# A decoder layer whose steps of attention and output projection are recorded in one block of manual order instead of two

## The chip, the core and the metric

The kernel runs on one core of a Trainium2 chip. A core has five engines with a queue of instructions each: PE (TensorE, matrix products; its weight loads are shown as PEld), DVE (VectorE), ACT (ScalarE), POOL (GpSimd) and SP (SyncE, which here only issues DMAs). An engine works its queue strictly in order and stands while the front instruction waits for a semaphore of another engine or of a DMA. The metric is the device time of one execution in microseconds (us).

## What is computed

One decoder layer in float32, 512 tokens of width 1024: a normalised input projection, two kinds of attention side by side, one output projection over both, a residual, and a SwiGLU feed-forward with its residual. Cut to its frame:

```python
for l in range(DEPTH):                                  # DEPTH = 1
    h = rms_norm(x, attn_pre_norm[l])
    mix = hybrid_mixer(h, ...)
    x = x + rms_norm(mix, attn_post_norm[l])
    h = rms_norm(x, ffn_pre_norm[l])
    f = (jax.nn.silu(h @ w_gate[l]) * (h @ w_up[l])) @ w_down[l]
    x = x + rms_norm(f, ffn_post_norm[l])

def hybrid_mixer(h, ...):
    dq, dk, dv, nq, kc, vc, ks, vs, kw, vw, gt = jnp.split(h @ w_in, ...)
    o_diff = ...        # 4 heads: difference of two causal softmaxes, then rms_norm
    o_nsa = nsa_attention(...)   # 8 heads: compressed, selected and window branch, mixed by gates
    return jnp.concatenate([o_diff, o_nsa], axis=-1) @ w_out
```

With 512 tokens the selected and the window branch of the second kind cover all causal keys.

## The kernel before

Every product is made to float32 accuracy from halves: a value is split into a high part (`h`, `hi`: ACT or POOL rounds it) and a low part (`l`, `lo`: DVE or POOL subtracts the high part from the value), and PE sums high x high, low x high and high x low. Tokens are worked in four blocks of 128.

The work is cut into small steps with names, and two tables of these names set the order in which the steps are recorded. `PLAN` holds the input projection and both attentions, head by head. Of a head of the second kind (`nsa_head`, names from `N0` to `N7`) the last steps are: `T` transposes the probabilities on PE (tile `tr`), `H` and `L` split them (`pth` on ACT, `ptl` on DVE), and `V1u` multiplies them with the values (`avs`, L1044, tile `avn`; `u` is 0, 1, 2, and unit 0 is the first key block, unit 1 the second, unit 2 the third and fourth). When the last matmul of `avn` is through, `O1` copies half of it (`avt`, ACT L1052), `O2` adds the two halves into `opair` (DVE L1058), `OH` makes the high part `oh` (ACT L1064) and `OL` the low part `ol` (POOL L1067). `D3OH` and `D3OL` do the same for head 3 of the first kind (ACT L958, POOL L974). `PLAN` ends with these steps of head 7.

`PLAN_NORM` holds what follows: the output projection in pieces (`mx20` is token block 2, row block 0 of the weight `w_out`: six matmuls `mix`, L1125, three for each half of the width), then for each token block its sum (`mixt`, DVE L1231), the norms and the residual `x` (ACT L1239, DVE L1254 to L1267), the scaled input of the feed-forward (`pre`, DVE L1271), its transposes on PE (`trh`, L1301) and the split of these (`x11h`, `x11l`, `x12h`, `x12l`). After it come the products of the feed-forward (`yz` and `x`, L1378), seven for eight by a scheme that multiplies sums of blocks, which is why DVE makes sums of weights first: `U1` (`e`, L1335), `U3` (`wraw`, L1342), `U2` (`e`, L1337), `U4` (`d`, L1340), then the low parts `wbl` and `wel` (L1363). Weights come by `load_w` (L267) into three buffers `wraw`; a load is issued by SP when the buffer's last reader is done.

`PLAN_NORM` begins with the loads of two weights and the pieces `mx20` and `mx30`, which need only attention heads that ended long before.

Each table is recorded inside a `manual_schedule()` of its own. Within such a block each engine gets its instructions in the order of the table. Where one block ends and the next begins, the two are not kept apart by anything but the data: the scheduler of the language puts the end of one and the start of the next into PE's queue as it sees fit. Between the two blocks the memory of the attention (`tctx`) is given back and the pools of the feed-forward are opened.

Of the kernel before, what the change touches and what calls it, by code (L numbers as in the profile page):

```python
# [245 lines left out]
def hybrid_block_kernel(  # L246
# [99 lines left out]
    ops = {}  # L346
# [813 lines left out]
        op(f"G{m}", mix_keep, m)  # L1160
    plan = PLAN.split()
    assert sorted(plan) == sorted(ops), set(plan) ^ set(ops)
    with tc.manual_schedule():
        for tok in plan:
            ops[tok]()
    tctx.close()
    A = ctx.enter_context(tc.tile_pool(name="a", bufs=1, side="right", reuse_waits="tile"))
    B = ctx.enter_context(tc.tile_pool(name="b", bufs=1, side="right", reuse_waits="tile"))
# [632 lines left out]
    plan, end = PLAN_NORM.split(), PLAN_END.split()  # L1801
    plan += [tok for _, tok in sorted(todo, key=lambda x: x[0]) if tok not in set(plan + end)] + end
    assert sorted(plan) == sorted(ops), set(plan) ^ set(ops)
    with tc.manual_schedule():
        for tok in plan:
            ops[tok]()


# [89 lines left out]
```

## Time and profile before

| what | value |
|---|---|
| three runs | 654.22, 1542.87 and 651.18 us; median 654.22 |
| profiled execution | 649.97 us, of which the span of instructions is 648.0 |
| granted clock of PE over the span | 0.995 |
| instructions | 11131, of which PE 4162 matmuls, DVE 955, ACT 780, POOL 151 |
| DMA | 98.42 MB, mean 152 GB/s |
| attention's last `opair` | 269.87 us from the span's start |
| feed-forward products on PE | 304 to 640 us |

The page shows one execution. Starts are counted from the span's start. "Idle before" is time in which an engine stood with its next instruction not yet released; the releaser named is the event that came last.

### The profile page before, as it was taken

How to read it: one execution, taken by the hardware profiler on the slowest of the kernel's cores; microseconds unless marked ns; L12 is line 12 of the kernel's file. 1: busy time of each engine (PE TensorE's matmuls, PEld its weight loads, DVE VectorE, ACT ScalarE, POOL GpSimd, SP SyncE). 2: the span in 40 equal slices, each digit the busy share in tenths (PEclk: the TensorE clock that was granted, in tenths of full speed). 3: DMA queues.
4: the chain of work that ended last, by engine and by line, in shares of the span. 5: the costliest groups of instructions: out<-in, count | busy, mean ns of one | idle time of the engine just before them, and what ended most of it. 6: DMA issues, size and time to landing. Idle time of an engine off the chain costs nothing.

```text
span 648.0 us, 11131 instructions
## 1 busy us (share of the span) xinstructions
PE 630.6 (97%) x4162; PEld 570.6 (88%) x4162; DVE 551.0 (85%) x955; ACT 374.3 (58%) x780; POOL 98.4 (15%) x151
## 2 busy tenths in 40 slices
PE   9999999999999999989999999999999999999995
PEld 6988787889998989868999999999999997778883
DVE  5799787688789776698999999988989999889886
ACT  7346545457787867557665735455554654657532
POOL 0200000006676787600000000000000000000000
PEclk9999999999999999989999999999999999999998
DMA  8467795257330321544235343334443365445722
GB/s 291 155 221 257 252 324 188 93 182 257 102 113 23 127 66 34 195 160 165 97 100 163 102 127 125 120 115 121 145 129 128 107 202 157 170 149 185 254 78 98
DMA packets 33045, 98.42 MB, mean 152 GB/s; under 512 B 4192, under 2 KB 5344, under 8 KB 32096
## 3 DMA queue, kind: packets, MB, share of 16 engines
q1 hardware_dynamic: 32992, 97.72, 45.1%
q8 instruction: 33, 0.54, 0.3%
q14 instruction: 20, 0.16, 0.1%
HBM read 82.10 MB, written 15.60 MB: 151 GB/s over the span
## 4 chain that ended last, share of the span: by engine, by line
PE 45%; DVE 8%; DMA 3%; ACT 1%; issue 1%; DVEq 0%; SPq 0%
PE yz L1378 27%; PE acc L1452 8%; PE x L1378 4%; PE acc L1600 3%; DMA wraw<-in_wd 2%; PE mix L1125 2%; DVE tl L1495 1%; DVE wraw L1469 1%; DVE wlo L1507 1%; DVE sl L1486 1%; DVE wraw L1471 1%; PE trh L1301 1%; DMA wraw<-in_wg 1%; ACT pre L1239 1%; DVE t L1475 1%
## 5 line engine op out<-in xcount | busy, mean ns | idle before, releaser
L848 ACT ACTIVATE p<-sc,nm 128x256 f32<-128x256 f32 (+3 forms) x96 | 50.1, 528 | 19.5 <-DVE nm L844 17.8
L844 DVE TENSOR_REDUCE nm<-sc 128x1 f32<-128x128 f32 (+3 forms) x96 | 43.3, 482 | 10.2 <-PE sc L840 6.9
L1378 PE MATMUL yz<-rope,wbh 128*128 128x256 f32 x352 | 49.1, 282 | 0.0
L1013 POOL TENSOR_TENSOR p<-p,l 128x256 f32<-128x256 f32 (+3 forms) x64 | 45.1, 729 | 0.9
L1378 PEld LDWEIGHTS yz<-rope,wbh 128*128 128x128 f32 x352 | 44.8, 188 | 0.3
L878 DVE TENSOR_TENSOR ptl<-tr,pth 128x384 fp32r<-128x384 f32 (+1 forms) x60 | 34.5, 594 | 8.7 <-ACT pth L875 8.1
L834 PE MATMUL sc<-kst,qst 128*128 128x384 f32 (+3 forms) x96 | 32.6, 357 | 2.9 <-DMA kst<-qk 2.1
L1355 ACT ACTIVATE weh<-e 128x1024 fp32r<-128x1024 f32 x22 | 23.3, 1057 | 19.7 <-DVE e L1337 17.0
L875 ACT ACTIVATE pth<-tr 128x384 fp32r<-128x384 f32 (+1 forms) x60 | 30.4, 526 | 6.6 <-PE tr L865 5.7
L835 PE MATMUL sc<-kst,qst 128*128 128x384 f32 (+3 forms) x96 | 30.9, 322 | 0.0
L1501 ACT ACTIVATE whi<-wraw 128x1024 fp32r<-128x1024 f32 x20 | 21.0, 1055 | 16.5 <-PE acc L1452 10.6
L1355 ACT ACTIVATE wbh<-wraw 128x1024 fp32r<-128x1024 f32 x22 | 23.1, 1056 | 11.5 <-DVE wraw L1342 11.4
L865 PE MATMUL tr<-ident,p 128*128 128x128 f32 x200 | 28.3, 274 | 0.0
L1363 DVE TENSOR_TENSOR wel<-e,weh 128x1024 fp32r<-128x1024 f32 x22 | 26.9, 1223 | 1.6 <-ACT weh L1355 1.6
L1363 DVE TENSOR_TENSOR wbl<-wraw,wbh 128x1024 fp32r<-128x1024 f32 x22 | 26.8, 1222 | 1.6 <-ACT wbh L1355 1.6
L1378 PE MATMUL yz<-rope,wbl 128*128 128x256 f32 x176 | 28.1, 282 | 0.0
L521 PE MATMUL fm<-xh,whi 128*128 128x512 f32 x112 | 28.0, 391 | 0.0
L1507 DVE TENSOR_TENSOR wlo<-wraw,whi 128x1024 fp32r<-128x1024 f32 x20 | 24.3, 1220 | 4.3 <-ACT whi L1501 4.3
L521 PE MATMUL fm<-xh,wlo 128*128 128x512 f32 x112 | 27.7, 390 | 0.0
L521 PE MATMUL fm<-xl,whi 128*128 128x512 f32 x112 | 27.7, 390 | 0.0
L1363 DVE TENSOR_TENSOR wlo<-wraw,whi 128x1024 fp32r<-128x1024 f32 x22 | 26.7, 1218 | 0.1
L1355 ACT ACTIVATE whi<-wraw 128x1024 fp32r<-128x1024 f32 x22 | 23.2, 1056 | 5.2 <-DMA wraw<-in_wg 4.7
(377 smaller groups left out, 1985.1 us busy)
## 6 DMA issues: line engine op xcount, KB each, us to landing
wraw<-in_wg SPq DMA_DIRECT2D x24, 512.0 KB, 3.6
wraw<-in_wu SPq DMA_DIRECT2D x22, 512.0 KB, 3.5
wraw<-in_wd SPq DMA_DIRECT2D x22, 512.0 KB, 4.0
wraw<-in_wf SPq DMA_DIRECT2D x14, 512.0 KB, 5.1
qk<-rope SPq DMA_DIRECT2D x7, 1024.0 KB, 4.9
kst<-qk SPq DMA_DIRECT2D x24, 256.0 KB, 3.8
wraw<-in_wo SPq DMA_DIRECT2D x8, 512.0 KB, 4.3
qst<-qk SPq DMA_DIRECT2D x16, 256.0 KB, 3.0
```

Of the source, the lines that this page charges most:

```text
L521: pe.matmul(st["fm", m], fms[m][w][:, k * P:(k + 1) * P], xx[k], start=(c == 0 and k == 0), stop=(c == 2 and k == NK - 1))
L834: pe.matmul(sv[i], lhs, kk[:, 0, :w], start=(n == 0), stop=False, skip_group_check=True)
L835: pe.matmul(sv[i], lhs, kk[:, 1, :w], start=False, stop=False, skip_group_check=True)
L844: dve.tensor_reduce(nm[i], sv[i], AX.X, OP.max, negate=True)
L848: act.activation(pp[i], sv[i], AF.Exp, bias=nm[i], accum_out=hs["l"][:, row, i:i + 1])
L878: dve.tensor_tensor(part(u, 1), tv[u], f32(part(u, 0)), OP.subtract)
L1013: pool.tensor_tensor(p, p, hs["l"][:, 1 + br, i:i + 1].to_broadcast(list(p.shape)), OP.mult)
L1355: act.activation(t[0], w[src], AF.Copy)
L1363: dve.tensor_tensor(t[1], W[f][PARTS[n][0]], f32(t[0]), OP.subtract)
L1378: pe.matmul(o, W[f][w][wi][:, k * P:(k + 1) * P], hop[h][hi][:, k * HS:(k + 1) * HS], start=(n < 3 and m == 0), stop=(m == 11), skip_group ...
L1452: pe.matmul(acc[t], a[x][:, t * P:(t + 1) * P], b[y], start=(first and n == 0), stop=(last and n == 2))
L1507: dve.tensor_tensor(lo, o["raw"], f32(o["w"][0]), OP.subtract)
```

## The change

The first `with tc.manual_schedule()` becomes a context of the whole function, so that it stays open to the kernel's end, and the second one is dropped. The tables, the steps and their code are the same.

```diff
     plan = PLAN.split()
     assert sorted(plan) == sorted(ops), set(plan) ^ set(ops)
-    with tc.manual_schedule():
-        for tok in plan:
-            ops[tok]()
+    ctx.enter_context(tc.manual_schedule())
+    for tok in plan:
+        ops[tok]()
     tctx.close()
...
     assert sorted(plan) == sorted(ops), set(plan) ^ set(ops)
-    with tc.manual_schedule():
-        for tok in plan:
-            ops[tok]()
+    for tok in plan:
+        ops[tok]()
```

What it does to the queues is seen only on PE, at the one place where the two tables meet. `avn` is the product of head 7 with the values (`vn_1541`, `vn_1573` and `vn_1551` are the values of the second, third and fourth key block), `mix` the output projection. PE's queue there before:

```order
L1125 MATMUL mix<-wl_432,oh_1985 128x512
L1044 MATMUL avn<-pth,vn_1541 128x384
L1125 MATMUL mix<-wh_428,oh_1985 128x512
L1125 MATMUL mix<-wh_428,ol_1986 128x512
L1125 MATMUL mix<-wl_469,oh_1985 128x512
L1044 MATMUL avn<-ptl,vn_1541 128x384
L1044 MATMUL avn<-pth,vn_1573 128x256
```

Ahead of these rows stand five more rows of `mix`, and behind them six, and then the last three of `avn`:

```order
L1044 MATMUL avn<-ptl,vn_1573 128x256
L1044 MATMUL avn<-pth,vn_1551 128x128
L1044 MATMUL avn<-ptl,vn_1551 128x128
L1125 MATMUL mix<-wh_3136,oh_3286 128x512
L1125 MATMUL mix<-wh_3136,ol_3287 128x512
```

PE's queue there now, from the spreading of head 3's norm (`rsb`) on:

```order
L953 MATMUL rsb<-ident,dr 128x128 x4
L1044 MATMUL avn<-pth,vn_1541 128x384
L1044 MATMUL avn<-ptl,vn_1541 128x384
L1044 MATMUL avn<-pth,vn_1573 128x256
L1044 MATMUL avn<-ptl,vn_1573 128x256
L1044 MATMUL avn<-pth,vn_1551 128x128
L1044 MATMUL avn<-ptl,vn_1551 128x128
L1125 MATMUL mix<-wh_428,oh_1985 128x512
L1125 MATMUL mix<-wh_428,ol_1986 128x512
```

The six `avn` now follow each other. The fifteen `mix` matmuls that stood ahead of and among them (six, three and six) come behind them, in the order they had. Everything behind is the same. The queues of DVE, ACT, POOL and SP hold the same instructions in the same order; here is DVE's, which reads what PE makes there:

```order
L972 TENSOR_TENSOR sq<-o_3499,rsb 128x512
L1058 TENSOR_TENSOR opair<-avn,avt 64x512
L1335 TENSOR_TENSOR e<-wraw 128x512
L1342 TENSOR_TENSOR wraw<-wraw 128x512
L1337 TENSOR_TENSOR e<-wraw,e 128x512
```

Nothing moved in DVE's rows. A few tiles take another buffer of the same size than before, and with it four waits name another instruction: `ol` of head 3 on POOL waits for the second `avn` of the six instead of the eighth `mix` matmul; `d` (L1340) waits also for a `mix` matmul of the piece `mx30`; and two loads deep in the feed-forward's second half exchange a wait for POOL.

## Prediction

> **What bounds the kernel now.** I read the page's table of engines first, then PE's own list of waits, then the chain of waits, and last the timelines of the engines around 260 to 310 us, where the change lies. Columns of a timeline row: start and duration in us, engine, line, operation, output<-input, shape, count, and in brackets the idle time ahead of it with its releaser.
>
> ```profile
> PE 630.6 (97%) x4162; PEld 570.6 (88%) x4162; DVE 551.0 (85%) x955; ACT 374.3 (58%) x780; POOL 98.4 (15%) x151
> ...
> PE trh L1301 <- ACT cols L1244: 2.4, 1, 2.4
> ...
> 286.03 1.82 PE L1301 MATMUL trh<-ident,pre 128*128 128x128 f32 x8 [2.44 <-ACT cols L1244]
> ```
>
> PE is busy 97% of the span, so a gain must come out of the little time in which PE stands, or in which it runs slowly. The longest single stand is the second row: 2.44 us ahead of the transposes `trh` of the first token block, ending at 286.03. This is 20 us behind the place that the change touches. The stand ends when DVE delivers `pre`; the operands come from DVE's queue, which is in one line from the end of attention to there:
>
> ```profile
> 263.75 1.00 DVE L878 TENSOR_TENSOR ptl<-tr,pth 128x384 fp32r<-128x384 f32 x2
> ...
> 269.87 0.68 DVE L1058 TENSOR_TENSOR opair<-avn,avt 64x512 f32<-64x512 f32 x1 [4.16 <-ACT avt L1052]
> 270.59 0.69 DVE L1335 TENSOR_TENSOR e<-wraw 128x512 f32<-128x512 f32 x1
> 271.37 1.77 DVE L1342 TENSOR_TENSOR wraw<-wraw 128x512 f32<-128x512 f32 x1
> ...
> 276.66 1.28 DVE L1231 TENSOR_TENSOR mixt<-mix,rope 128x512 f32<-128x512 f32 x2
> ...
> 279.36 0.69 DVE L1335 TENSOR_TENSOR e<-wraw 128x512 f32<-128x512 f32 x1 [0.16 <-DMA wraw<-in_wg]
> ...
> 285.13 0.75 DVE L1271 SCALAR_TENSOR_TENSOR pre<-x,cols,gain 128x512 f32<-128x512 f32 x1
> ...
> 285.86 0.74 DVE L1271 SCALAR_TENSOR_TENSOR pre<-x,cols,gain 128x512 f32<-128x512 f32 x1
> ```
>
> DVE stands 4.16 us ahead of `opair` (269.87) and then has work with hardly a break until `pre` (the two halves end at 285.88 and 286.60). So DVE's start at 269.87 decides when PE may go on at 286.03. What it stands for is ACT's `avt`, and that waits for the last `avn` matmul on PE:
>
> ```profile
> 265.75 0.63 ACT L958 ACTIVATE oh<-sq 128x512 fp32r<-128x512 f32 x1 [1.31 <-DVE sq L972]
> 269.24 0.60 ACT L1052 ACTIVATE avt<-avn 64x512 f32<-64x512 f32 x1 [2.86 <-PE avn L1044]
> ...
> 264.68 0.47 PE L1125 MATMUL mix<-wh,oh 128*128 128x512 f32 x1
> ...
> 266.15 0.34 PE L1044 MATMUL avn<-pth,vn 128*128 128x384 f32 x1
> 266.32 0.39 PE L1125 MATMUL mix<-wh,oh 128*128 128x512 f32 x1
> ...
> 268.70 0.28 PE L1044 MATMUL avn<-ptl,vn 128*128 128x256 f32 x1
> ...
> 268.98 0.45 PE L1125 MATMUL mix<-wh,oh 128*128 128x512 f32 x1
> ...
> 272.68 0.47 PE L1125 MATMUL mix<-wh,ol 128*128 128x512 f32 x1
> ```
>
> PE itself never stands here: between the six remaining `avn` matmuls it does 15 `mix` matmuls of the output projection.
>
> **The change, step by step.** No instruction is added or removed. On PE the six `avn` matmuls of head 7 move ahead of the 15 `mix` matmuls that stood among them; the order on DVE, ACT, POOL and in SP's queue stays row for row, so no DMA is moved.
>
> *PE's order itself: 0.* The first of the six holds PE 0.17 us (266.15 to 266.32), the last three 0.28 (268.70 to 268.98); with the two between, of the same shapes (0.17 and 0.12), about 0.74. They run 264.68 to 265.4, their last result is there at about 265.6, and the 15 `mix` matmuls go later by what the `avn` before them take, 0.74 at most. At 268.98 both orders have done the same work. The block needs the second `ptl` of DVE, done at 263.75 + 1.00 = 264.75; it is wanted at about 265.1, so PE does not stand. This cover is 0.4 us wide; before, the wanted time was 268.70.
>
> *`avt` and `opair`: 2.8 us earlier.* ACT has `oh` in front of `avt` (265.75 + 0.63 = 266.38), which is now what is late. `avt` goes at about 266.4 instead of 269.24, and `opair` at 267.0 to 267.7 instead of 269.87 to 270.55.
>
> *DVE against POOL: 2.6 to 4.0.* Two subtractions of weights follow `opair`, `e` and `wraw`, each with both inputs in SBUF.
>
> ```profile
> 265.45 1.30 POOL L1099 TENSOR_TENSOR wl<-wraw,wh 128x512 fp32r<-128x512 f32 x1
> 267.10 1.29 POOL L974 TENSOR_TENSOR ol<-sq,oh 128x512 fp32r<-128x512 f32 x1 [0.35 <-PE mix L1125]
> 271.30 1.29 POOL L1067 TENSOR_TENSOR ol<-opair,oh 128x512 fp32r<-128x512 f32 x1 [2.92 <-ACT oh L1064]
> ...
> 290.63 0.68 DVE L1342 TENSOR_TENSOR wraw<-wraw 128x512 f32<-128x512 f32 x1
> ...
> wraw<-in_wu SPq DMA_DIRECT2D x1, 512.0 KB, 3.8
> ```
>
> `wraw` takes 0.68 us where POOL is idle (290.63) and 1.77 where POOL began an `ol` 0.07 before it (271.30); it ended at 273.14, 0.55 behind POOL. So one of the two stood for the other. Now the first `ol` starts when `wl` ends (266.78; its wait for PE falls on an `avn` that is long done) and ends at 268.07, and `e` would start at 267.7: it ends at 268.65. The second `ol` follows `opair` by 0.75 (270.55 to 271.30), so it is ready at 268.45, ahead of `wraw`: 268.65 to 269.94, and `wraw` ends at 270.5, 2.6 earlier than 273.14. If nothing were blocked, `wraw` would end at 269.1, 4.0 earlier. I take 2.6, since the one row that shows the meeting shows the block. The Trainium skill, "SBUF — State Buffer", section "Who interferes with whom", says that a DVE instruction with two SBUF inputs and a GpSimd instruction that reads SBUF take a shared port in turn, and that the one issued second waits for the whole of the first; by that rule two blocks stand here instead of one, and the gain of this step is 2.6; without it 4.0. The row of 1.77 us agrees with it. The weight load `wraw<-in_wu` that `e` needs (the first row of DMA above, from issue to landing 3.8 us) was issued at 262.93 and is there at 266.7, ahead of 267.7.
>
> *What else could hold DVE until `pre`.* `mixt` reads PE's sum of the first token block. Its first half ends with the matmul behind 272.68, so near 273.3: `mixt` can come 3.3 earlier than 276.66 and no more. With 2.6 it starts at 274.06. The `e` of 279.36 waits for a load that is issued when DVE's buffer is free:
>
> ```profile
> 275.63 3.63 DMA wraw<-in_wg
> ...
> wraw<-in_wu SPq DMA_DIRECT2D x1, 512.0 KB, 7.2
> ```
>
> Issued 2.6 earlier, at 273.0, it lands at 276.65; DVE wants it at 276.6. The load ahead of it (issued 266.78, 7.2 us) is through at 273.98. At most 0.1 lost here. So `pre` ends 2.6 earlier, its halves at 283.3 and 284.0.
>
> *The stand of PE: 2.44 plus its slow clock.*
>
> ```profile
> 287.50 0.78 PE L1125 MATMUL mix<-whi,oh 128*128 128x512 f32 x1
> ...
> 289.92 0.39 PE L1125 MATMUL mix<-wh,oh 128*128 128x512 f32 x1
> ...
> 295.37 1.04 PE L1301 MATMUL trh<-ident,pre 128*128 128x128 f32 x8
> ...
> 288.00:289.00 1.00, 1.00 (x4) 0.73 (x3) 0.93 (x3) 1.00 (x1) 0.00 (x0) 0.50 0.00 0
> ...
> 72.10 0.41 PE L834 MATMUL sc<-kst,qst 128*128 128x384 f32 x1 [0.90 <-DMA kst<-qk]
> ...
> 72.00:73.00 1.00, 0.90 (x7) 0.78 (x7) 0.13 (x1) 0.79 (x2) 0.00 (x0) 1.00 0.87 262
> ```
>
> PE comes to `trh` at 283.5 (286.03 - 2.44). The first half of `pre` is there, the second 0.1 late: `trh` ends near 284.4 instead of 287.50, 3.1 earlier. Behind the stand PE was granted half its clock (the number behind POOL's bracket in a window's row: 0.50 in 288 to 289): six `mix` matmuls took 2.42 us (287.50 to 289.92), while the next 24 took 5.45 (to 295.37), 0.227 each. Without the stand six take 1.36, another 1.06. PE is then 4.1 early. A stand of 0.90 (at 72.10) left the clock at 1.00.
>
> *Back to DVE, and what is late next.*
>
> ```profile
> 294.88 0.60 ACT L1239 ACTIVATE pre<-mix 128x512 f32<-128x512 f32 x1 [1.33 <-PE mix L1125]
> ...
> 296.35 0.16 DVE L1241 TENSOR_TENSOR cols<-cols 128x1 f32<-128x1 f32 x1 [0.68 <-ACT pre L1239]
> ...
> 306.40 0.68 DVE L1294 TENSOR_TENSOR x12l<-trh,x12h 128x512 fp32r<-128x512 f32 x1
> ...
> 307.14 0.74 PE L1378 MATMUL x<-x12l,whi 128*128 128x256 f32 x4 [0.19 <-DVE x12l L1294]
> ...
> 318.51 15.77 PE yz L1378 x132
> ...
> 507.47 5.26 PE yz L1378 x44
> ```
>
> DVE's 0.68 us at 296.35 is a wait for ACT, and ACT's for PE's sum of the third block. PE is 4.1 early there and DVE 2.6, so these 0.68 go and DVE is 3.3 early from then on. `x12l` ends at 307.08 - 3.3 = 303.8, and PE, which has come 4.1 early, stands about 0.9 for it: 3.3 of its 4.1 are left. From 307.14 to 512 the chain runs over PE alone (its first long and its last piece are the last two rows), and all that feeds it is released by the same engines; the 3.3 are kept.
>
> **Sum.** 2.6 (DVE's shift) + 0.7 (a stand of DVE that goes) = 3.3 us. The bounds: 4.0 if POOL and DVE never meet (3.3 + 0.7), 4.1 as the most that PE can win, 0 if something between holds everything where it is. The profiled execution took 649.97 us, so 646.7 in its place. It is the fastest of those shown; with the runs of 651.18 and 654.22 the mean is 651.8 (the run of 1542.87 is far from all others and left out). The profiled one lies 4.3 below the median of 654.22. What is to be forecast is a run like these, so I set the 3.3 against 651.8: 648.5.
>
> **Rivals.**
> The gain is halved by a new slow stretch of the clock. PE now stands 0.9 us at `x<-x12l`. For it: 2.44 us halved the clock. Against it: 0.90 at 72.10 did not. The price is that of the stretch at 286: from 286.03 to 289.92 PE took 3.89 us for work of 0.79 + 1.36, 1.7 more. Then 3.3 - 1.7 = 1.6 are left, 650.2. The Trainium skill, "TensorE: Matmul & The Clock Gate", Part 1, says that the clock is halved after an idle window of about 3.4 us; by it no stand here would do that and this rival falls away, but 2.44 us did in this trace, so it keeps its chance.
>
> No change. The load at 275.63 is bound by traffic and not by its issue, lands at 279.26 as before, and `e` and all behind it stay. For it: the load ahead took 7.2 us and not 3.8. Against it: that one is through at 273.98. Then 651.8.
>
> Slower. PE stands in front of the six `avn`, since nothing else may pass them now: each us that `ptl` comes later than 265.1 delays all `mix` by one us. With a stand of 2.4 us the slow clock adds 1.7, 4.1 in all against 3.3 won: from there it decides, and gives 651.8 + 0.8 = 652.6. For it: the cover is only 0.4 us. Against it: both `ptl` are ended at 264.75, and nothing that the change moves lies in front of them.
>
> **How the numbers follow.** My forecast 0.62, the halved gain 0.18, no change 0.13, slower 0.07. The predicted time is 648.5. The range: at the low end 649.97 - 4.1 = 645.9, rounded out to 645.5; at the high end the slowest ordinary run with nothing won, 654.2; it holds the first three cases with the spread of the runs. Two per cent, about what a measurement of this kernel can tell from no change, are 13 us; none of the cases reaches that, so within 2% gets 0.95, and 0.03 faster and 0.02 slower stand for what I have not seen.
>
> **What would show it.** `avt` at about 266.4, `opair` at 267.0; two long DVE subtractions next to POOL's two `ol`, the second ending near 270.5; `mixt` near 274.0; no stand of PE ahead of `trh`, or one under 0.5 us, and a clock of 1.00 from 284 to 290; DVE without its 0.68 at `cols` L1241; PE's stand for `x12l` grown to about 0.9; the gain unchanged from there to the end. The prediction is wrong if PE stands in front of `avn`, if the second load of `in_wg` lands later than 277, or if the gain at 310 us is not found again at 512 and at the end.

## The result and the profile after

The changed kernel takes 649.07 us (median of 20 runs, 643.98 to 656.84), the kernel before 651.92 (20 runs, 649.65 to 1542.87). The ratio is 0.9936, with a 95% interval of 0.9909 to 0.9963: about 4.2 us less, between 2.4 and 5.9. This ratio leaves out the five slowest runs of the changed kernel (654.15 to 656.84 us, over 1.5% above its fastest) and of the kernel before only that of 1542.87; with the five the means are 650.07 and 652.41, 2.3 us apart, and by drawing the runs again at random the difference lies between about 0.4 and 4.3. So a gain is shown, and its size by the run times only to within some 2 us. The prediction was 648.5, 3.3 less than the mean that it started from.

The profiled execution of the changed kernel took 652.87 us (span 650.8), 2.9 *more* than that of the kernel before (649.97). So the two profiles can't be set beside each other by their totals; why not is the first thing to read. First PE's row of the page's table of engines, then two rows of PE's list of waits (total in us, times, longest), for the kernel after:

```profile
PE 632.9 (97%) x4162; PEld 573.1 (88%) x4162; DVE 550.6 (85%) x955; ACT 374.6 (58%) x780; POOL 98.4 (15%) x151
...
PE sc L834 <- DMA kst<-qk: 4.6, 3, 2.7
...
PE x L1378 <- DVE x12l L1294: 0.5, 1, 0.5
```

The longest wait of before, `trh` for 2.4 us, is gone from the list. But PE waits 4.6 us for loads of keys (`kst<-qk`), far ahead of the change; in the profile of before they cost it 2.1. Stands like these, and pieces of time at half clock behind them (the last section shows one), shift all that follows. The spreading of head 3's norm (`rsb`), PE's last work ahead of the change, began at 263.87 before and begins at 270.34 here: 6.47 later. All times below are therefore counted from the start of `rsb`, or set back by 6.47. The timelines around the change, after:

```profile
270.34 1.05 PE L953 MATMUL rsb<-ident,dr 128*128 128x128 f32 x8
271.15 0.42 PE L1044 MATMUL avn<-pth,vn 128*128 128x384 f32 x1
...
271.88 0.27 PE L1044 MATMUL avn<-ptl,vn 128*128 128x128 f32 x1
271.99 0.44 PE L1125 MATMUL mix<-wh,oh 128*128 128x512 f32 x1
...
272.22 0.63 ACT L958 ACTIVATE oh<-sq 128x512 fp32r<-128x512 f32 x1 [1.31 <-DVE sq L972]
272.88 0.60 ACT L1052 ACTIVATE avt<-avn 64x512 f32<-64x512 f32 x1
...
273.50 0.69 DVE L1058 TENSOR_TENSOR opair<-avn,avt 64x512 f32<-64x512 f32 x1 [1.32 <-ACT avt L1052]
274.22 0.76 DVE L1335 TENSOR_TENSOR e<-wraw 128x512 f32<-128x512 f32 x1
275.07 1.71 DVE L1342 TENSOR_TENSOR wraw<-wraw 128x512 f32<-128x512 f32 x1
...
280.37 1.28 DVE L1231 TENSOR_TENSOR mixt<-mix,rope 128x512 f32<-128x512 f32 x2
...
282.82 0.69 DVE L1335 TENSOR_TENSOR e<-wraw 128x512 f32<-128x512 f32 x1
...
273.15 1.29 POOL L974 TENSOR_TENSOR ol<-sq,oh 128x512 fp32r<-128x512 f32 x1
274.94 1.30 POOL L1067 TENSOR_TENSOR ol<-opair,oh 128x512 fp32r<-128x512 f32 x1 [0.50 <-ACT oh L1064]
```

`avt` no longer shows a wait for PE: the six `avn` begin 0.81 us behind the start of `rsb` and are done when ACT ends `oh`. DVE stands 1.32 us ahead of `opair` where it stood 4.16. `wraw` ends at 276.78, 6.44 behind the start of `rsb`; before it ended 9.27 behind it (273.14 - 263.87). So DVE has won 2.83. Further back, in the timelines and in two windows (the number behind POOL's bracket is the granted clock):

```profile
289.76 1.04 PE L1301 MATMUL trh<-ident,pre 128*128 128x128 f32 x8
...
299.04 0.15 DVE L1241 TENSOR_TENSOR cols<-cols 128x1 f32<-128x1 f32 x1
...
309.05 0.68 DVE L1294 TENSOR_TENSOR x12l<-trh,x12h 128x512 fp32r<-128x512 f32 x1
...
309.78 0.74 PE L1378 MATMUL x<-x12l,whi 128*128 128x256 f32 x4 [0.54 <-DVE x12l L1294]
```

```profile
286.00:288.00 2.00, 2.00 (x11) 1.65 (x10) 1.98 (x6) 1.83 (x5) 0.00 (x0) 1.00 0.56 229
288.00:290.00 2.00, 2.00 (x12) 1.64 (x11) 1.90 (x8) 1.35 (x4) 0.00 (x0) 1.00 0.46 154
```

PE does not stand at `trh`, the clock stays at 1.00, and DVE's 0.68 at `cols` is gone. From the start of `rsb` to that of the second `x12l` on DVE it was 42.53 us before (306.40 - 263.87), and is 38.71 here (309.05 - 270.34): 3.82 won. This distance is what the experiments compare; it is called *the stretch* below. Three pieces of the chain of waits show that almost nothing is given back later:

```profile
321.13 15.77 PE yz L1378 x132
...
510.08 5.26 PE yz L1378 x44
...
634.70 2.78 PE acc L1600 x12
```

The first two began at 318.51 and 507.47 before, 2.62 and 2.61 earlier on the clock of the trace, which is 6.47 less 3.85. The third is PE's last piece in the chain, and before it stood here:

```profile
631.81 2.78 PE acc L1600 x12
```

That is 2.89 earlier, so 3.58 of the 3.85 are left at the end. What is missing goes near 580 us, where PE stands 0.89 us for ACT's `c` (L1522) in this execution and 0.38 before; why it stands longer stays open.

### The profile page after: what moved, and what is told of

Read it like the earlier page. It is cut to its first block, busy times and chain, and to the rows that moved or that the text cites. A ratio compares the mean times of both kernels' runs of the same rounds, so it can differ in the third digit from the quotient of the medians.

```text
span 650.8 us, 11132 instructions
## 1 busy us (share of the span) xinstructions
PE 632.9 (97%) x4162; PEld 573.1 (88%) x4162; DVE 550.6 (85%) x955; ACT 374.6 (58%) x780; POOL 98.4 (15%) x151
## 4 chain that ended last, share of the span: by engine, by line
PE 43%; DVE 10%; DMA 2%; issue 2%; ACT 1%; DVEq 0%; SPq 0%
PE yz L1378 27%; PE acc L1452 9%; PE x L1378 4%; PE acc L1600 3%; DMA wraw<-in_wd 2%; DVE tl L1495 1%; DVE wraw L1469 1%; DVE wlo L1507 1%; DVE sl L1486 1%; DVE wraw L1471 1%; DVE wlo L1363 1%; DVE t L1475 1%; DVE pre L1271 0%; DVE u L1261 0%; DVE wbl L1363 0%
## 5 line engine op out<-in xcount | busy, mean ns | idle before, releaser
L834 PE MATMUL sc<-kst,qst 128*128 128x384 f32 (+3 forms) x96 | 33.7, 367 | 4.6 <-DMA kst<-qk 4.6
L835 PE MATMUL sc<-kst,qst 128*128 128x384 f32 (+3 forms) x96 | 31.9, 333 | 0.0
```

The costliest lines, as they stand in the source:

```text
L834: pe.matmul(sv[i], lhs, kk[:, 0, :w], start=(n == 0), stop=False, skip_group_check=True)
L835: pe.matmul(sv[i], lhs, kk[:, 1, :w], start=False, stop=False, skip_group_check=True)
```

## The experiments

Theory: the gain is the order on PE. `avt` comes earlier, DVE with it, the stand of PE at `trh` goes, and the slow clock that this stand brings goes with it. The rivals were other buffers and waits that come with one block, and a slow clock that belongs to the one profiled execution. The stretch in every profiled execution, in us:

| kernel | stretch | stand of PE at `trh` | clock fell behind it |
|---|---|---|---|
| before | 42.53 | 2.44 | yes |
| before, again (b_again, b_again2) | 42.45, 42.59 | 2.33, 2.30 | yes, yes |
| one block, PE's old order (e1) | 41.61 | 2.32 | no |
| the same again (e1_again, e1_again2) | 42.88, 42.76 | 2.56, 2.66 | yes, yes |
| before, stand filled (e2) | 41.79 | 0.47 | no |
| six `avn` still later (e6) | 43.57 | 2.33 | no |
| changed kernel, and again | 38.71, 38.75 | none | no |
| `avt` still earlier (e3) | 38.99 | none | no |
| both `ol` on DVE (e4) | 38.55 | none | no |

In the recorded expectations Z is the stretch. A is the time from the matmul behind `rsb` to the first `x<-x12l` on PE, and lies 0.07 or 0.08 below the stretch in every row: 42.46 before, 38.63 in the changed kernel.

### One block with PE's old order

The changed kernel, with the steps of the seam recorded in the order that PE's queue had before. `mix_three` is the three matmuls of one half of a piece of the output projection, `one(j, t)` the `avn` matmul of key block j. Their definitions are left out here, and so are the places further on that pass over what is already recorded.

```diff
...
-        ops[tok]()
+        if tok == "N7V12":
+            one = av_ones[7]
+            mix_three(2, 0, 0), mix_three(2, 0, 1), one(1, 0), mix_three(3, 0, 0), one(1, 1), one(2, 0)
+            mix_three(3, 0, 1), mix_three(0, 2, 0), one(2, 1), one(3, 0), one(3, 1)
+        elif tok != "N7V11":
+            ops[tok]()
...
```

> One block of manual order as in the changed kernel, but PE's queue at the seam is recorded in the old order: six mix, avn, three mix, two avn, six mix, three avn. Every queue then reads as before. Let A be the time from the matmul behind rsb to the first x<-x12l on PE (before 264.68 to 307.14 = 42.5 us; changed 271.15 to 309.78 = 38.6). Theory (the order of the six avn is all that counts): A = 42.5 within 0.3, PE stands about 2.4 us ahead of trh, ratio to before 1.000 within 0.004. Rival (the gain comes of the other buffers that the single block gives out, or of the four waits that name another instruction): A = 38.6 and a ratio near 0.994.

Measured in five rounds: a ratio to before of 1.001 (0.9978 to 1.0043), 653.41 us. The timeline of its profile:

```profile
266.11 1.05 PE L953 MATMUL rsb<-ident,dr 128*128 128x128 f32 x8
...
272.11 0.68 DVE L1066 TENSOR_TENSOR opair<-avn,avt 64x512 f32<-64x512 f32 x1 [4.16 <-ACT avt L1060]
...
288.15 1.29 PE L1327 MATMUL trh<-ident,pre 128*128 128x128 f32 x8 [2.32 <-ACT cols L1270]
...
307.72 0.68 DVE L1320 TENSOR_TENSOR x12l<-trh,x12h 128x512 fp32r<-128x512 f32 x1
```

DVE's 4.16 us and PE's stand are back to within 0.12. The single block as such is worth nothing that these runs can tell; the order is the gain. But the clock did not fall in this execution, and the stretch is 0.92 shorter than before's: A is 41.54, outside the 42.5 within 0.3 that the theory expected, though far from the rival's 38.6. So the slow clock is not a fixed consequence of the stand, which the next runs take up.

### The slow clock alone

The kernel before, with nine 128x512 matmuls in the place where PE stands. They write a buffer that `trh` overwrites, so the result is not changed.

```diff
             trs[i] = wide("trh")
+            for _ in range(9 if i == 0 else 0):
+                pe.matmul(trs[0][0], oth[5][:, :P], wos[5][0][0], start=True, stop=True)
```

> The kernel before, with nine matmuls more (128x512, into the buffer that trh overwrites, so that nothing of the result changes) in the place where PE stands ahead of trh: 9 x 0.227 = 2.0 us of the 2.44. DVE is not moved. Theory (the stand costs PE's clock as well, and of that clock DVE gets back only the 0.68 us that it waits at cols L1241): clock 1.00 from 286 to 290 on before's scale, the six mix behind trh in 1.4 us instead of 2.4, no wait of DVE at cols L1241, A = 42.5 - 0.7 = 41.8. Rival one (the slow clock costs nothing in the end): A = 42.5. Rival two (all that PE gains counts): A = 42.5 - 1.5 = 41.0.

```profile
262.88 1.05 PE L953 MATMUL rsb<-ident,dr 128*128 128x128 f32 x8
...
285.11 1.29 PE L1303 MATMUL trh<-ident,pre 128*128 128x128 f32 x8 [0.47 <-ACT cols L1244]
...
294.66 0.15 DVE L1241 TENSOR_TENSOR cols<-cols 128x1 f32<-128x1 f32 x1
...
304.67 0.68 DVE L1294 TENSOR_TENSOR x12l<-trh,x12h 128x512 fp32r<-128x512 f32 x1
```

PE comes to `trh` as late as before and DVE's `pre` comes when it did; only the clock is kept. DVE's 0.68 wait at `cols` goes, and the stretch is 41.79, 0.74 shorter than before's 42.53 (A is 41.72, as the theory had it). That is the price of the slow clock at the end of the stretch, and it agrees with e1, whose clock stayed up by itself. The remaining 3 us between 41.7 and 38.7 are the order.

### `avt` still earlier

The changed table with `N7O1` (`avt`) ahead of head 3's `oh` (`D3OH`), so that ACT does it first.

```diff
-D3O3 D3ML D3OH D3OL N7V12 N7O1 N7O2 N7OH N7OL
+D3O3 D3ML N7V12 N7O1 D3OH D3OL N7O2 N7OH N7OL
```

> The changed kernel with avt of head 7 put ahead of head 3's oh in ACT's queue. avt and opair come about 0.8 us earlier than in the changed kernel (avt 0.95 us behind the start of the first of the six avn instead of 1.73). Theory (DVE and POOL take turns where both read SBUF twice): POOL's two ol follow each other without a break, e and wraw stand for them, wraw ends no more than 0.2 us earlier, A between 38.4 and 39.0. Rival (they do not block each other; wraw's long row had another reason): wraw ends 0.8 us earlier than in the changed kernel, A = 38.1 or less.

```profile
273.93 1.69 DVE L1335 TENSOR_TENSOR e<-wraw 128x512 f32<-128x512 f32 x1
275.71 1.61 DVE L1342 TENSOR_TENSOR wraw<-wraw 128x512 f32<-128x512 f32 x1
...
273.77 1.30 POOL L974 TENSOR_TENSOR ol<-sq,oh 128x512 fp32r<-128x512 f32 x1 [0.27 <-ACT oh L958]
275.03 1.75 POOL L1067 TENSOR_TENSOR ol<-opair,oh 128x512 fp32r<-128x512 f32 x1
```

`avt` came 1.91 us behind the start of `rsb` (270.67 in this run) instead of 2.54, and `opair` 0.62 earlier. Nothing was won. POOL's `ol` is now issued 0.16 ahead of `e` and `e` ends 0.55 behind it (275.62 to 275.07); POOL's second `ol`, begun while `e` runs, is drawn out to 1.75; `wraw` ends 0.54 behind that. `wraw` ends 6.65 behind `rsb` where it was 6.44, and the stretch is 38.99, 0.28 longer. Two engines take turns here, and an earlier start only changes whose turn it is. The Trainium skill, "SBUF — State Buffer", section "Who interferes with whom", states such an exclusive lock; the trace agrees, and shows that POOL pays as well (1.75 for 1.30).

How much of such a difference is chance was read from the changed kernel itself, profiled once more:

> The changed kernel once more, unaltered, for the spread of A from one execution to the next and for what comes ahead of the seam. Theory (the gain lies wholly between the six avn and x12l; the executions differ ahead of it): A = 38.6 within 0.2, the start of the seam anywhere between 263 and 273 us. Rival (A itself spreads by a microsecond or more, so that one profile each says little): A outside 38.1 to 39.1.

38.75 against 38.71, and the three profiles of the kernel before differ by 0.14 at most. The 0.28 of e3 is twice that; a difference under 0.2 says little.

### The six `avn` still later

All six behind 24 `mix` matmuls, in the changed kernel.

The additions that this kernel shares with e1 are left out.

```diff
+EARLY_MIX = ((2, 0), (3, 0), (0, 2), (0, 3))
...
+        if tok == "N7V12":
+            one = av_ones[7]
+            for i, k in EARLY_MIX:
+                mix_three(i, k, 0), mix_three(i, k, 1)
+            for j, n in ((1, 0), (1, 1), (2, 0), (2, 1), (3, 0), (3, 1)):
+                one(j, n)
...
```

> The kernel before in one block, but with the six avn behind 24 mix matmuls (token blocks 2 and 3 of one row block, block 0 of two) instead of among the first 15: their end comes about 1.95 us later than before. Let Z be the time from the start of the row of rsb on PE to the start of the second x12l on DVE (before 42.5, of which 0.8 is the slow clock; old order in one block 41.6; changed kernel 38.7 and 38.8). Theory (DVE's queue starts when avn ends and carries the delay one for one): Z = 41.7 + 1.95 = 43.6 with PE's clock at 1.00, 44.4 if the stand halves it; opair 8.0 us behind the row of rsb instead of 6.0. Rival (below some point the place of avn is hidden by what DVE waits for anyway): Z near 41.7.

```profile
269.04 1.05 PE L954 MATMUL rsb<-ident,dr 128*128 128x128 f32 x8
...
277.05 0.68 DVE L1067 TENSOR_TENSOR opair<-avn,avt 64x512 f32<-64x512 f32 x1 [6.16 <-ACT avt L1061]
...
293.04 1.29 PE L1328 MATMUL trh<-ident,pre 128*128 128x128 f32 x8 [2.33 <-ACT cols L1271]
...
312.61 0.68 DVE L1321 TENSOR_TENSOR x12l<-trh,x12h 128x512 fp32r<-128x512 f32 x1
```

`opair` starts 8.01 behind `rsb` (before 6.00, old order in one block 6.00) and the stretch is 43.57 with the clock kept, against 41.61: 2.01 later in, 1.96 later out. The chain from `avt` over DVE to `trh` passed this delay on one for one. PE's stand at `trh` did not grow, since PE now stood another 0.7 and 0.8 us earlier, for `oh` and `ol`.

### Both `ol` on DVE

If POOL's two subtractions are in the way, DVE can do them itself.

```diff
-D3O3 D3ML D3OH D3OL N7V12 N7O1 N7O2 N7OH N7OL
+D3O3 D3ML N7V12 N7O1 D3OH N7O2 D3OL N7OH N7OL
...
-            OL=lambda: pool.tensor_tensor(otl[h], hs["sq"], f32(oth[h]), OP.subtract))
+            OL=lambda: (dve if h == 3 else pool).tensor_tensor(otl[h], hs["sq"], f32(oth[h]), OP.subtract))
...
-            pool.tensor_tensor(otl[kt], opair[kt], f32(oth[kt]), OP.subtract)
+            (dve if h == 7 else pool).tensor_tensor(otl[kt], opair[kt], f32(oth[kt]), OP.subtract)
```

> The changed kernel with avt ahead of head 3's oh on ACT, and with the two low parts ol of heads 3 and 7 (the two POOL instructions that e and wraw meet) made on DVE between opair and e. POOL is then idle when e and wraw run. Theory (the shared port): e and wraw take 0.69 each, wraw ends about 5.9 us behind the row of rsb instead of 6.4, the DVE queue comes 0.5 to 0.6 earlier to mixt, which PE lets start at 9.4 at the earliest; Z = 38.1 to 38.3, time 0.5 us below the changed kernel, ratio to before near 0.993. Rival (two instructions more on DVE cost as much as the meetings did): Z = 38.7 or more.

```profile
270.76 0.69 DVE L974 TENSOR_TENSOR ol<-sq,oh 128x512 fp32r<-128x512 f32 x1
271.43 0.69 DVE L1067 TENSOR_TENSOR ol<-opair,oh 128x512 fp32r<-128x512 f32 x1
272.04 0.69 DVE L1335 TENSOR_TENSOR e<-wraw 128x512 f32<-128x512 f32 x1
272.81 0.69 DVE L1342 TENSOR_TENSOR wraw<-wraw 128x512 f32<-128x512 f32 x1
...
279.82 0.69 DVE L1335 TENSOR_TENSOR e<-wraw 128x512 f32<-128x512 f32 x1 [0.19 <-DMA wraw<-in_wg]
```

With POOL idle all four subtractions take 0.69 each, and `wraw` ends 5.99 behind `rsb` (267.51 in this run) instead of 6.44. Of these 0.45 the stretch keeps at most 0.16 to 0.20 (38.55 against 38.71 and 38.75), hardly more than profiles of one kernel differ by; the 38.1 to 38.3 of the theory were missed. The rest was not kept: the second `e` now stands 0.19 for its load, which the chain of this run shows as 3.66 us from 276.07 on, and the load is issued only when DVE has done with the buffer. Over five rounds the ratio to before is 0.9944 (0.9913 to 0.9976), 648.41 us: no different from the changed kernel's 0.9936. No variant tried beats the changed kernel by what can be measured.

### Does the clock fall each time?

The kernel before twice more, and e1 twice more, each for one profile.

> The kernel before once more, for its slow clock behind trh. Theory (whether the stand of 2.4 us halves PE's clock is a matter of the execution, since the old order in one block stood 2.3 us and kept 1.00): Z = 41.6 with the clock at 1.00 behind trh, or 42.5 with 0.50. Rival (the kernel before always falls to half, and the old order in one block differs in something else): 42.5 and 0.50.

> The kernel before a third time, the same question: Z = 41.6 at a clock of 1.00 or 42.5 at 0.50; the rival again only the latter.

In both the clock fell (42.45 and 42.59), which spoke for the rival: that e1 keeps the clock and the kernel before does not. So e1 was run twice more.

> The old order in one block once more, for the clock behind the stand ahead of trh. The kernel before fell to half in three executions of three, the old order in one block (two kernels) in none of two. Theory (the fall depends on where the stand lies in a window that runs by itself, so it comes in some executions of either): Z = 41.6 with 1.00 or 42.5 with 0.50, and in one of the two repeats 42.5. Rival (the old order in one block never falls, so it differs from the kernel before in something that is not seen in the order of its queues): 41.6 and 1.00 in both.

> The same a third time: Z = 42.5 with a clock of 0.50 in this or in the repeat ahead of it by the theory, 41.6 and 1.00 in both by the rival.

It fell in both, and the stretch is as long as before's (42.88 and 42.76; of it 0.28 and 0.38 are a wait of DVE for the second load of `in_wg`). The clock falls in some executions of either kernel: in five of the seven with a stand of 2.3 to 2.7 us. When it falls is seen in the timeline and the windows of the second repetition of before:

```profile
288.74 1.29 PE L1301 MATMUL trh<-ident,pre 128*128 128x128 f32 x8 [2.30 <-ACT cols L1244]
```

```profile
289.00:290.00 1.00, 0.99 (x9) 0.76 (x8) 1.00 (x2) 0.60 (x1) 0.00 (x0) 0.97 0.90 348
290.00:291.00 1.00, 1.00 (x4) 0.77 (x3) 0.90 (x5) 0.36 (x1) 0.00 (x0) 0.50 0.01 4
...
293.00:294.00 1.00, 1.00 (x5) 0.78 (x5) 1.00 (x3) 0.94 (x5) 0.00 (x0) 0.82 0.91 377
```

The stand ended at 288.74, and PE then ran at full clock for more than a microsecond. A mean of 0.97 in 289 to 290 is 0.06 us at half clock, 0.82 in 293 to 294 is 0.36: the slow time lasts from 289.94 to 293.36.

## Why the prediction came out right, step by step

The time alone tests little: the range, 645.5 to 654.2 us, would have held no change as well. What was tested are the steps.

**PE's order and `avt`: right.** The six `avn` begin 0.81 us behind the start of `rsb`, as foretold (264.68 against 263.87), and PE does not stand for `ptl`. `avt` was foretold for 266.4 and came at 272.88 - 6.47 = 266.41; `opair` for 267.0, and came at 267.03.

**DVE against POOL, 2.6: right in kind, 0.2 too small.** It was foretold that `e` would stand for POOL's first `ol` and `wraw` for its second, with `wraw` ending at 270.5. `e` took 0.76 and `wraw` 1.71, and `wraw` ended at 270.31: 2.83 earlier. e3 and e4 show that the meeting with POOL is real; with POOL out of the way (and `avt` first) `wraw` came another 0.45 earlier. The other bound of the prediction, 4.0 without any block, was not tested by itself: e4 has no block, but two instructions more on DVE, and its `wraw` ends 3.28 earlier than before's.

**The load of `in_wg`: 0.1 lost was allowed, 0.16 was won.** The wait at the second `e` disappeared, and DVE's shift grew from 2.83 to 3.01 ((279.36 - 263.87) - (282.82 - 270.34)). The cover is thin: in e4, where DVE is another 0.45 earlier, that wait returns.

**The stand at `trh` and the clock: right for the profiled execution, wrong as a property of the kernel.** The prediction took the slow clock as part of what the stand of 2.44 costs. It comes in five of seven executions. What it is worth in the end is 0.7 to 1.0 (e2 against before 0.74; e1 against before 0.92 and against its own repetitions 1.27 and 1.15, of which 0.28 and 0.38 are the wait for a load).

**The sum, 3.3: 3.8 in the profiled pair.** The two terms were 2.6 and 0.7; they measured 3.01 and 0.77 (DVE's shift at `cols` L1241 is 3.78: 296.35 - 263.87 less 299.04 - 270.34). PE's stand at `x<-x12l` was to grow to 0.9 and grew to 0.54, for the same reason: DVE came 0.5 earlier than foretold. Where the clock does not fall behind `trh`, the change is worth 41.61 - 38.71 = 2.9. Both lie in the measured 2.4 to 5.9, and in the 0.4 to 4.3 of all runs. That the forecast of 3.3 lies between the two is in part luck: 0.7 of it hung on a fall that not every execution has, and `wraw` and the load gave 0.4 more than the 2.6 foretold.

**The rivals.** The halved gain fell: a stand of 0.54 left the clock at 1.00, as it did in e1, e2 and e6. No change fell: the load was issued at 279.34, 2.76 earlier against `rsb`, and `e` no longer waited for it. The gain was to be found again at 512 and at the end: at 510 it is whole, at the end 3.58 of 3.85. Slower fell: `avn` is not waited for.

**The total.** The forecast of 648.5 was set against a mean over runs, not against the one profile, and that was needed: the start of `rsb` lies between 262.88 and 271.99 us over the twelve profiled executions, while the change is worth 3 to 4. By the two profiles' totals it would have been read as a loss of 2.9. What the front part's length goes with was read afterwards, from windows of 1 us: a mean clock of c is 2 x (1 - c) us at half clock. The sums from 8 us to `rsb`:

| time at half clock ahead of `rsb` | start of `rsb` |
|---|---|
| 0.0 us (e2, before, b_again) | 262.88, 263.87, 264.89 |
| 3.4 us (e1, b_again2, e1_again2, e4) | 266.11, 266.71, 267.12, 267.51 |
| 6.8 us (a_again, e6) | 267.81, 269.04 |
| 10.2 to 10.3 us (after, e3, e1_again) | 270.34, 270.67, 271.99 |

The clock falls for 3.4 us at a time, and the twelve executions fall into groups by how often. The profile of before had no fall ahead of the seam, that of after three. At half clock 10.2 us hold at most 5.1 us less work, and the loads of keys cost 2.5 us more of standing (4.6 against 2.1): together at most 7.6, of which 6.47 were seen. No experiment was made on it: why a load comes late in one execution and not in another stays open, and the profiles are too few to say whether the change makes the falls rarer or more frequent. The timed runs show no large difference: the mean granted clock is 0.993 over the 20 of the changed kernel, and 0.992 over either set of 17 runs of the kernel before that was taken beside e1 and e4.

## What to carry to other kernels

When a stretch of time is won on an engine that waits (DVE here, 4.16 us), follow its queue to the next place where the busiest engine waits for it; the gain is made there, less what the engines beside it take (POOL's two `ol`) and the next load allows. Where two blocks of a manual order meet, look at the queue at the seam: the order there is nobody's, and six matmuls of 0.8 us in all cost 2.9 us by standing behind fifteen others. Compare two profiles from a common instruction just ahead of the change, and the kernels by many runs: how often the clock falls on the way, and how late loads come, moved a single profile by more than the effect did here.

## What the runs showed of the hardware

While PE has work, time at half clock comes in pieces of one size here. Behind `trh` it followed a stand of 2.30 to 2.66 us in five of seven executions, and began between 0.0 and 1.2 us behind the stand's end; it lasted 3.4 us each time, whatever the stand. The same is seen far ahead of the change, here in the timeline and the windows of the kernel after:

```profile
105.82 0.41 PE L834 MATMUL sc<-kst,qst 128*128 128x384 f32 x1 [2.66 <-DMA kst<-qk]
```

```profile
107.00:108.00 1.00, 1.00 (x4) 0.69 (x3) 0.08 (x1) 0.92 (x1) 0.00 (x0) 0.51 0.91 361
...
110.00:111.00 1.00, 1.00 (x8) 1.00 (x8) 0.81 (x5) 0.86 (x3) 0.00 (x0) 0.79 0.00 0
```

By the same reckoning it lasts from 107.02 to 110.42, 3.40 us, and begins 1.2 behind the stand. A stand of 1.65 us for the keys was followed by such a piece in one repetition of before (3.4 us from 105.6 on) and by none in the other; the shortest with a single piece behind it was 1.45 us (e1_again, where the piece begins 2.2 us later). In e6 two pieces follow each other without a gap, 6.8 us from 104.9 on; e3 and e1_again show such a pair as well. And in the kernel after one begins at 28.5 with no stand of more than 0.2 us in the 4 us ahead of it, behind sixteen matmuls of one column each.

The Trainium skill, "TensorE: Matmul & The Clock Gate", Part 1, tells of a window of about 3.4 us that runs freely and does not begin anew when a kernel starts. The length, the multiples of it, and the beginning that varies against the stand fit that. It also says that the clock is halved after an idle window of that length; here the clock fell behind 1.45 to 2.7 us of standing, in some executions and not in others, and the measurement decides. That a window counts as idle with some work in it would explain both, and no run here puts that to the test.

Moving a DVE instruction nearer to a POOL instruction cost both of them time: 1.69 and 1.61 us on DVE where 0.69 is the price alone, and 1.75 on POOL for 1.30.
